# Seven quarter products for five of the 22 pairs of an MLP's first product

## The chip, the cores and the metric

One Trainium2 chip, one of its cores. The metric is device microseconds of one execution, from the kernel's first instruction to its last output. Engines are called by these names: TensorE (PE in the profile, with PEld for its weight loads), VectorE (DVE), ScalarE (ACT), GpSimd (POOL), SyncE (SP, which issues DMAs).

## The reference, cut to what matters

One layer of an encoder over 512 tokens of 1024 channels: four token mixers, a cross-attention, then a gated MLP. The change is in the MLP:

```python
hf = _rms_norm(x, norm_ffn_pre)                       # (512, 1024)
u = _dwconv_causal(hf @ w_up, ffn_dw) + ffn_dw_b      # w_up (1024, 5632), width-3 taps over tokens
u_g, u_v = jnp.split(u, 2, axis=-1)                   # 2816 gate, 2816 value channels
yff = (jax.nn.silu(u_g) * u_v) @ w_down               # w_down (2816, 1024)
x = x + _rms_norm(yff, norm_ffn_post)
```

All is float32, and the products keep more than one pass of TensorE would: each operand x is split into a rounded high part and a low part x - high, and a product is the sum of three (high·high, high·low, low·high).

## The kernel before, in words

The kernel writes out its work as a list of jobs (`all_jobs`), which `run_blocks` takes in order: a job loads a block of weights (`load_raw`, on SP's queue, two buffers `wr`), splits it (`split_weights`: ScalarE casts the high part `wh`, L190; VectorE subtracts for the low part `wl`, L191; four buffers each) and runs a body of matmuls. Three jobs are fetched ahead of the body that runs. The program's own scheduler then sets each engine's order, so an engine's rows are not in the order of the code.

**The first MLP product** (`up_jobs`). The 2816 gate and 2816 value channels are 22 pairs of blocks of 128 channels; block n is pair j = n // 2, gate or value i = n % 2. A block is 8 steps k of 128 input channels by 3 passes = 24 matmuls of 128x128 weights against 128x512 tokens (`channel_major`, `mm3`; every matmul is recorded at L232), summed in one PSUM bank. Then `done`: ScalarE starts the width-3 convolution out of PSUM (L1557), VectorE adds the other two taps (L594, `taps`), and after the value block ScalarE takes a tanh (L1561) and VectorE makes silu(gate)·value out of it in two instructions (L1562, L1564). The first four blocks run on 256 tokens at a time, since the second half of the tokens is normalized last (`norm_task`, which turns each 128 tokens to channels on TensorE, L236, and splits them into `hth` and `htl`, L155 and L156).

**The second MLP product** (`down_jobs`) already takes seven products of quarters for eight, in two phases over 11 double pairs q. For it GpSimd sums quarters of the activations (`activation_sums`, L566 to L569, four instructions for each q, as soon as pair 2q + 1 is done), and VectorE sums quarters of the weights during the first product (class `Sums`, L542 to L545, four instructions for each q), loading from and storing to DRAM on ScalarE's DMA queue (L538, L549).

The banks of PSUM: two each of `mm`, `av`, `sc`, `tr`. The first product uses `mm` and `av` in turn, and `sc` for two of the first four blocks; `tr` and `sc` are otherwise free while it runs.

Of the kernel before, what the change touches and what calls it, by code (L numbers as in the profile page):

```python
# [17 lines left out]
F32 = mybir.dt.float32  # L18
# [20 lines left out]
HALF_SHIFT = 16  # L39
BIG = -float(2.0 ** 100)  # L40
# [43 lines left out]
def hybrid_layer(ctx: ExitStack, tc: tile.TileContext, a: dict, out: bass.AP):  # L84
# [146 lines left out]
    def matmul(ps, lhs, rhs, start, stop):  # L231
        PE.matmul(ps, lhs, rhs, start=start, stop=stop)  # L232
        bg.clock += max(int(math.prod(rhs.shape[1:])), 256) * 0.00042
# [52 lines left out]
    def to_channels(y_t, act, t):  # L286

        sl = slice(t * P, (t + 1) * P)
        for half in range(2):
# [4 lines left out]
            split(ps.rearrange("p (k c) -> p k c", k=4), act[0][:, ks, sl], act[1][:, ks, sl])  # L294

# [994 lines left out]
    def norm_task(t, ms, scaled, src, gain, act):  # L1290
# [5 lines left out]
        if act is ns.hx:  # L1296
            load_x(t + 2)
        y_t = normed(ns.work, ns.out[t], [gain], ns.work.tile([P, D], F32, tag="nt", name="nt", bufs=2), ns.normed)
        yield 2.5, 7.0
        to_channels(y_t, act, t)  # L1300
# [7 lines left out]
    def open_mix_out():  # L1308
        close(m2)
        ns.res_, resp = new_pool("res", False)  # L1310
        ns.xr, ns.normed = None, []
        ns.out = [resp.tile([P, D], F32, name=f"res{t}") for t in range(NT)]
# [113 lines left out]
    def open_cross():  # L1426
        close(ns.mix_)
        ns.xp_, ns.xp = new_pool("xp", True)
        ns.xq = (ns.xp.tile([P, 4, S], F32R, name="xqh"), ns.xp.tile([P, 4, S], F32R, name="xql"))
        ns.pt = {}  # L1430
        ns.xp_gap = True
# [72 lines left out]
    def open_cross_out():  # L1504
# [5 lines left out]
        ns.hf = new_ht()  # L1510

# [26 lines left out]
    def open_ffn():  # L1538
        bg.drain("n1")
        close(ns.work_)  # L1540
# [4 lines left out]
        ns.quart = [(ns.fp.tile([P, 4, S // 2], F32, tag=f"qa{q}", name="qa"),  # L1545
                     ns.fp.tile([P, 3, S // 2], F32, tag=f"qb{q}", name="qb")) for q in range(NF // 2)]
        ns.post = ns.fp.tile([P, D], F32, name="g_ffn")
        G.dma_start(ns.post, a["norm_ffn_post"][0].partition_broadcast(P))

    def up_jobs():  # L1550
        st, held = {}, []

        def done(j, i, ps):
            if i == 0:
                st[j] = ns.fp.tile([P, 2, S], F32, tag="c", name="c", bufs=2)
            c, ch = st[j], i * NF + j
            st["first"] = A.activation(c[:, i], ps, AF.Identity, bias=pc("fb", ch), scale=pc("fdw2", ch)).ins  # L1557
            st["taps"] = taps(c[:, i], ps, lambda k: pc("fdw01", k * 44 + ch), 3).ins
            if i == 1:
                th = ns.fp.tile([P, S], F32, tag="th", name="th")  # L1560
                A.activation(th, c[:, 0], AF.Tanh, scale=0.5)  # L1561
                V.scalar_tensor_tensor(th, th, 1.0, c[:, 0], ALU.add, ALU.mult)  # L1562
                x = ns.quart[j // 2]
                V.scalar_tensor_tensor(x[j % 2][:, 0:2].rearrange("p a b -> p (a b)"), th, 0.5, c[:, 1],  # L1564
                                       ALU.mult, ALU.mult)
                if j % 2:
                    activation_sums(*x, G)


        for n in range(2 * NF):  # L1570
            def body(hi, lo, n=n):
                j, i = divmod(n, 2)
                if n > 3:
                    ps = bank()
                    channel_major(ps, (hi, lo), ns.hf)
                    done(j, i, ps)

                    q = n // 3 - 2
                    if 0 <= q < NF // 2:
                        with tc.issue_after(st["taps" if n % 3 == 0 else "first"]):  # L1580
                            (ns.sums.add, ns.sums.store, ns.sums.load)[n % 3](q + 2 * (n % 3 == 2))
                    return
                if n == 0:
                    bg.drain("n0")
                ps = bank(("mm", "sc")[n % 2])
                (channel_major if n else by_pass)(ps, (hi, lo), ns.hf, slice(0, S // 2))
# [233 lines left out]
```

## Time and profile before

| | |
|---|---|
| median of 3 runs | 1055.36 us (1055.04 to 1056.72) |
| the profiled execution, its own time | 1055.79 us |
| span of its profile | 1054.0 us |
| mean granted clock of TensorE | 0.997 |
| first MLP product, by TensorE | 695.8 to about 946 us |
| second MLP product and the end | about 946 to 1054 us |
| DMA during the first product (750 to 900 us) | 225 GB/s, 69% of the DMA engines' time |

A row of an engine's timeline has the start in us, the length in us, engine, line, operation, what is written and read, the shape, and in brackets how long the engine was idle before and what ended that. Instructions of one engine overlap a little: the next starts before the one ahead of it has ended. In the chain of waits a row is a start, a length and what ran; x24 stands for 24 matmuls in a row. Times in the text are from the span's start.

### The profile page before, as it was taken

The numbers are of one execution on the slowest core, as the hardware profiler recorded it, in microseconds if no ns is written. First come the engines' busy times: TensorE is split into PE (matmuls) and PEld (weight loads), VectorE is DVE, ScalarE is ACT, GpSimd is POOL, SyncE is SP. The second block draws the span as 40 slices with busy tenths as digits, with TensorE's granted clock in tenths as the row PEclk, the third lists the DMA queues.
The fourth block names the chain that finished last, engine by engine and source line by source line (L and its number), as shares of the span: only waits on it lengthen the run. The fifth ranks groups of instructions, "written<-read, shape, count | busy, mean of one in ns | idle before, by whom it ended". The sixth has DMA issues, their size and how long they took to land.

```text
span 1054.0 us, 14559 instructions
## 1 busy us (share of the span) xinstructions
PE 1041.7 (99%) x5295; PEld 886.8 (84%) x5295; DVE 807.1 (77%) x1280; ACT 501.9 (48%) x823; POOL 184.3 (17%) x309
## 2 busy tenths in 40 slices
PE   9999999999999999999999999999999999999996
PEld 8888888888888988888888899998888888888885
DVE  6899997668667467867487798777878777777795
ACT  5322222277465365655444566554333333355661
POOL 4000000300231233433011031121112111111001
PEclk9999999999999999999999999999999999999998
DMA  8854434742342353232359644135576676626662
GB/s 276 282 168 102 103 100 142 193 109 81 116 140 82 100 161 101 80 100 85 96 172 284 207 132 126 60 111 190 186 243 229 214 233 215 196 81 211 210 188 80
DMA packets 165373, 163.08 MB, mean 155 GB/s; under 512 B 6527, under 2 KB 136172, under 8 KB 165045
## 3 DMA queue, kind: packets, MB, share of 16 engines
q1 hardware_dynamic: 152995, 119.91, 38.0%
q0 software_dynamic: 5824, 19.03, 6.2%
q10 hardware_dynamic: 6482, 23.21, 5.7%
q8 instruction: 42, 0.69, 0.3%
q14 instruction: 30, 0.25, 0.1%
HBM read 139.03 MB, written 23.09 MB: 154 GB/s over the span
## 4 chain that ended last, share of the span: by engine, by line
PE 99%; DVE 0%; ACT 0%; issue 0%; POOL 0%; POOLq 0%; DVEq 0%; ACTq 0%
PE ps_mm L232 51%; PE ps_av L232 31%; PE ps_sc L232 8%; PE ps_tr L232 4%; PE ps_tr L236 2%; PE ps_mm L442 1%; PE ps_av L442 1%; PE ps_mm L384 0%; PE ps_sc L389 0%; DVE o L1710 0%; PE ps_tr L426 0%; POOL st_m L270 0%; POOLq L1816 0%; ACT hth L155 0%; ACT hth L432 0%
## 5 line engine op out<-in xcount | busy, mean ns | idle before, releaser
L190 ACT CAST wh<-wr 128x1024 fp32r<-128x1024 f32 (+1 forms) x142 | 148.8, 1049 | 273.3 <-PE ps_mm L232 175.0
L191 DVE TENSOR_TENSOR wl<-wr,wh 128x1024 fp32r<-128x1024 f32 (+1 forms) x142 | 178.5, 1258 | 79.0 <-ACT wh L190 78.8
L232 PE MATMUL ps_mm<-hth,wh 128*128 128x512 f32 (+1 forms) x592 | 221.1, 380 | 0.2 <-ACT hth L155 0.2
L232 PE MATMUL ps_mm<-htl,wh 128*128 128x512 f32 (+1 forms) x592 | 220.7, 379 | 0.0
L232 PE MATMUL ps_mm<-hth,wl 128*128 128x512 f32 (+1 forms) x592 | 220.6, 379 | 0.0
L232 PE MATMUL ps_av<-htl,wh 128*128 128x512 f32 (+1 forms) x352 | 131.8, 374 | 0.0
L232 PE MATMUL ps_av<-hth,wh 128*128 128x512 f32 (+1 forms) x352 | 131.8, 374 | 0.0
L232 PE MATMUL ps_av<-hth,wl 128*128 128x512 f32 (+1 forms) x352 | 131.6, 374 | 0.0
L232 PEld LDWEIGHTS ps_mm<-hth,wh 128*128 128x128 f32 x592 | 109.6, 188 | 20.4 <-ACT hth L155 0.8
L232 PEld LDWEIGHTS ps_mm<-hth,wl 128*128 128x128 f32 x592 | 109.5, 188 | 20.1
L232 PEld LDWEIGHTS ps_mm<-htl,wh 128*128 128x128 f32 x592 | 109.6, 188 | 19.7
L665 DVE SCALAR_TENSOR_TENSOR y<-y,par,y 128x482 f32<-128x482 f32 (+29 forms) x120 | 83.3, 735 | 0.1
L232 PEld LDWEIGHTS ps_av<-hth,wl 128*128 128x128 f32 x352 | 66.1, 188 | 11.9
L232 PEld LDWEIGHTS ps_av<-hth,wh 128*128 128x128 f32 x352 | 66.2, 188 | 11.8
L232 PEld LDWEIGHTS ps_av<-htl,wh 128*128 128x128 f32 x352 | 66.0, 188 | 11.7
L1613 DVE TENSOR_TENSOR wl<-dw,wh 128x1024 fp32r<-128x1024 f32 x32 | 40.2, 1262 | 13.3 <-ACT wh L1612 13.1
L1612 ACT CAST wh<-dw 128x1024 fp32r<-128x1024 f32 x32 | 33.4, 1051 | 23.4 <-PE ps_tr L232 7.9
L1058 POOL TENSOR_SCALAR fbias<-ck,cq 128x128 f32<-128x128 f32 (+3 forms) x32 | 28.2, 888 | 63.0 <-DVE st L1065 59.7
L1561 ACT ACTIVATE th<-c 128x512 f32<-128x512 f32 x22 | 13.9, 632 | 48.0 <-DVE c L594 48.0
L155 ACT CAST pth<-ps_tr 128x512 fp32r<-128x512 f32 (+3 forms) x56 | 23.5, 448 | 24.7 <-PE ps_tr L236 24.6
L594 DVE SCALAR_TENSOR_TENSOR c<-ps_mm,par,c 128x510 f32<-128x510 f32 (+1 forms) x44 | 32.8, 744 | 0.7
L156 DVE TENSOR_TENSOR ptl<-ps_tr,pth 128x512 fp32r<-128x512 f32 (+3 forms) x56 | 27.5, 512 | 5.9 <-ACT pth L155 5.4
(493 smaller groups left out, 2132.5 us busy)
## 6 DMA issues: line engine op xcount, KB each, us to landing
wr<-in_w_up SPq DMA_DIRECT2D x44, 512.0 KB
wr<-in_w_in SPq DMA_DIRECT2D x38, 512.0 KB
wr<-in_w_gate SPq DMA_DIRECT2D x32, 512.0 KB
wp<-in_w_down ACTq DMA_DIRECT2D x22, 512.0 KB
sums<-wp ACTq DMA_DIRECT2D x22, 512.0 KB
dw<-sums SPq DMA_DIRECT2D x44, 256.0 KB
wr<-in_w_branch SPq DMA_DIRECT2D x16, 512.0 KB
wide<-in_w_out SPq DMA_DIRECT2D x12, 512.0 KB
```

What stands on the lines that cost most here:

```text
L155: A.copy(hi, ps)
L156: V.tensor_tensor(lo, ps, hi.bitcast(F32), ALU.subtract)
L190: order(A.copy(hi, raw[:, :n]))
L191: low.tensor_tensor(lo, raw[:, :n], hi.bitcast(F32), ALU.subtract)
L232: PE.matmul(ps, lhs, rhs, start=start, stop=stop)
L236: PE.transpose(ps, x, ident[:n, :n])
L442: keep(PE.matmul(banks[c][:, :S // 2], w[p == 1][:, k, c * P:(c + 1) * P], ht[p == 2][:, i * 4 + k, :S // 2], start=(i, p, k) == (0, 0, 0) ...
L594: ins = V.scalar_tensor_tensor(dst[:, s:], src[:, :S - s], w(k), dst[:, s:], ALU.mult, ALU.add)
L665: ins = V.scalar_tensor_tensor(dst[:, s:], src[:, :S - s], pc("conv_dw", k * 4 + j), dst[:, s:], ALU.mult, ALU.add)
L1058: G.tensor_scalar(bias[:, :w], ck[j][:, :w], -1.0, cq[:, qt, head:head + 1], ALU.mult, ALU.add)
L1612: A.copy(hi, x)
L1613: V.tensor_tensor(lo, x, hi.bitcast(F32), ALU.subtract)
```

## The change

**Pairs 5, 8, 11, 14 and 17** (`SEVEN_AT`) are computed in another way (`seven_jobs`). The pair's weights are seen as two rows, gate (A11, A12) and value (A21, A22), each cut into halves of 4 steps k; the tokens as four quarters B, cut by channel halves and token halves. Seven products of a weights' quarter with a tokens' quarter give the pair, with sums S1 to S4 of the weights and T1 to T4 of the tokens. A product is 4 steps by 3 passes = 12 matmuls against 256 tokens, into `sc` and `tr`; four of the seven go on adding into the same bank after ScalarE copied out the sum so far. The pair after (6, 9, 12, 15, 18) is done in the old way, its matmuls woven between the seven products, and pairs 7, 10, 13 and 16 stand between.

For it are added, for each of the five pairs: VectorE sums S1 to S4 (4 instructions of 128x512), one more split of 128x1024 (S1, S2) and one of 128x512 (S4), three additions out of PSUM of 128x256, and four copies out of PSUM of 128x256 on ScalarE. The splits of the pair's own two blocks stay, of (A11, A12) and of (S3, A22). Its raw weights come into a ring of 7 buffers (`dw`) that the sums of `w_down` use too; before, those had 4.

**The tokens' terms.** `norm_task` now also copies the turned tokens out of PSUM (`plain`, ScalarE, two copies of 128x512 for each of the four token tiles), and VectorE makes T1 to T4 from them (`token_terms`, 4 instructions of 128x1024) and splits them (`split_terms`, four more and four casts). T1 to T4 stand where the residual stood, so each of its four tiles goes to DRAM on SP's queue (`kept`, 512 KB each) and comes back during the second product (`reload`).

**Smaller edits.** For every pair, silu on ScalarE and one multiplication on VectorE take the place of tanh and two; ScalarE loads another function table once for it. The sums of `w_down` go through GpSimd's DMA queue in place of ScalarE's. GpSimd's sums of activations all come after pair 18 (`quart_sums`). The splits of the activations in the second product are two instructions of half the size in place of one.

```diff
+SEVEN_AT = (5, 8, 11, 14, 17)
...
     split(ps.rearrange("p (k c) -> p k c", k=4), act[0][:, ks, sl], act[1][:, ks, sl])
+    if plain is not None:
+        A.copy(plain[half][:, :, sl], ps.rearrange("p (k c) -> p k c", k=4))
...
+    def token_terms():
+        b11, b12, b21, b22 = (ns.plain[k][:, :, i * S // 2:(i + 1) * S // 2] for k in range(2) for i in range(2))
+        ns.terms = t1, t2, t3, t4 = [term_tile(i) for i in range(4)]
+        V.tensor_tensor(t1, b12, b11, ALU.subtract)
+        V.tensor_tensor(t2, b22, t1, ALU.subtract)
+        V.tensor_tensor(t3, b22, b12, ALU.subtract)
+        V.tensor_tensor(t4, b21, t2, ALU.subtract)
...
-                th = ns.fp.tile([P, S], F32, tag="th", name="th")
-                A.activation(th, c[:, 0], AF.Tanh, scale=0.5)
-                V.scalar_tensor_tensor(th, th, 1.0, c[:, 0], ALU.add, ALU.mult)
...
-                V.scalar_tensor_tensor(x[j % 2][:, 0:2].rearrange("p a b -> p (a b)"), th, 0.5, c[:, 1],
-                                       ALU.mult, ALU.mult)
+            A.activation(c[:, 0], c[:, 0], AF.Silu)
+            V.tensor_tensor(ns.quart[j // 2][:, j % 2 * 2:j % 2 * 2 + 2].rearrange("p a b -> p (a b)"), c[:, 0],
+                            c[:, 1], ALU.mult)
...
+            ns.sums = Sums(w_down, NF // 2, lambda: ring(name="wp"), G, "sums")
...
+            def first_weights():
+                weights(("A11", "A12"), g)
+                with tc.issue_after(st["taps"]):
+                    V.tensor_tensor(su[:, :S], v[:, :S], v[:, S:], ALU.add)
+                V.tensor_tensor(su[:, S:], su[:, :S], g[:, :S], ALU.subtract)
+                V.tensor_tensor(v[:, :S], g[:, :S], v[:, :S], ALU.subtract)
+                V.tensor_tensor(s4, g[:, S:], su[:, S:], ALU.subtract)
...
+            def first(_):
+                product(x["x"], "A11", old(0, 0))
+                A.copy(u[:, 0, 0], x["x"][:, :S // 2])
+                product(x["w"], "A12", old(1, 0))
+                add(u[:, 0, 0], x["w"])
+            def gate_first(hi, lo):
+                x["n"] = bank(), (hi, lo)
+                half_sums(*x["n"], range(4))
+            def second(_):
+                product(x["x"], "S2", ns.terms[1], False)
+                A.copy(kept["u"][:, 1, 0], x["x"][:, :S // 2])
+            def third(_):
+                product(x["v"], "S3", ns.terms[2])
+                half_sums(*x["n"], range(4, NK))
+                done(n, 0, x["n"][0])
+                product(x["x"], "S1", ns.terms[0], False)
+                A.copy(u[:, 1, 1], x["x"][:, :S // 2])
+                add(u[:, 1, 1], x["v"])
+            def value(hi, lo):
+                half_sums(ps, (hi, lo), range(4))
+                product(x["x"], "S4", old(1, 1), False)
+                A.copy(u[:, 0, 1], x["x"][:, :S // 2])
+                half_sums(ps, (hi, lo), range(4, NK))
+                done(n, 1, ps)
+                product(x["v"], "A22", ns.terms[3], False)
+                add(u[:, 1, 0], x["v"])
+                for i in range(2):
+                    first_and_taps(c, j, i, u[:, i].rearrange("p a b -> p (a b)"))
+                gated(c, j)
...
+            split_to(hi[:, :S], lo[:, :S], flat(ns.quart[q][:, 2 * phase:2 * phase + 2]))
+            split_to(hi[:, S:], lo[:, S:], new)
...
+            if (phase, q, job) == (1, 2, 0):
+                reload()
```

How instructions stand on VectorE in the middle of the first product, before (`wl<-wr` is the low part of a block's weights, `c` the convolution, `th` and `qb` the gate, `wp` the sums of `w_down`):

```order
L1562 SCALAR_TENSOR_TENSOR th<-th,c 128x512
L191 TENSOR_TENSOR wl<-wr,wh 128x1024
L594 SCALAR_TENSOR_TENSOR c<-ps_av,par_403,c 128x510
L594 SCALAR_TENSOR_TENSOR c<-ps_av,par_403,c 128x511
L542 TENSOR_TENSOR wp<-wp 128x512
L1564 SCALAR_TENSOR_TENSOR qb<-th,c 128x512
L543 TENSOR_TENSOR wp<-wp 128x512
L544 TENSOR_TENSOR wp<-wp 128x512
```

And at such a place now (`su`, `wv`, `s_8109` are the sums S1 to S4, `u` the additions out of PSUM):

```order
L1693 TENSOR_TENSOR su<-wv 128x512
L192 TENSOR_TENSOR wl<-wr,wh 128x1024
L1686 TENSOR_TENSOR u<-u,ps_sc 128x256
L546 TENSOR_TENSOR wp<-wp 128x512
L1694 TENSOR_TENSOR su<-su,wg 128x512
L1695 TENSOR_TENSOR wv<-wg,wv 128x512
L547 TENSOR_TENSOR wp<-wp 128x512
L192 TENSOR_TENSOR wl<-wr,wh 128x1024
L1696 TENSOR_TENSOR s_8109<-wg,su 128x512
L597 SCALAR_TENSOR_TENSOR c<-ps_av,par_403,c 128x510
L548 TENSOR_TENSOR wp<-wp 128x512
L597 SCALAR_TENSOR_TENSOR c<-u,par_403,c 128x510
```

Sums S1 to S4 and additions have come between the splits and the taps; a stretch of three pairs, which is one of the five and the two behind it, is 38 instructions on VectorE.

On VectorE at the start of the MLP, behind the last token tile's split, stand now the terms T1 to T4 (`t_7000` and on) ahead of the next blocks' low parts, and their splits (`t_7139`) between the first taps:

```order
L1575 TENSOR_TENSOR t_7002<-plain 128x1024
L1574 TENSOR_TENSOR t_7001<-plain,t_7000 128x1024
L1576 TENSOR_TENSOR t_7003<-plain,t_7001 128x1024
L192 TENSOR_TENSOR wl<-wr,wh 128x1024 x2
L597 SCALAR_TENSOR_TENSOR c<-ps_mm,par_403,c 128x510
L597 SCALAR_TENSOR_TENSOR c<-ps_sc,par_403,c 128x510
L157 TENSOR_TENSOR t_7139<-t_7000,t_7138 128x1024
```

Before, the two `wl` came straight behind the last token tile's split.

On TensorE, in a stretch of seven products (`t_7146` is T3, `t_7142` is T2; the rows of 128x512 into `ps_mm` are the neighbour pair's gate block):

```order
L233 MATMUL ps_mm<-hth,wl 128x512
L233 MATMUL ps_sc<-t_7146,wh 128x256
L233 MATMUL ps_sc<-t_7147,wh 128x256
L233 MATMUL ps_mm<-hth,wh 128x512
L233 MATMUL ps_mm<-htl,wh 128x512
L233 MATMUL ps_mm<-hth,wl 128x512
L233 MATMUL ps_sc<-t_7142,wh 128x256
```

Where there were 24 matmuls of 512 columns of one block after the other, runs of 256 columns now alternate with runs of 512: one such stretch turns from 256 columns to 512 six times.

More of the change, by code (lines that the diff above doesn't have):

```diff
@@ L1599, in down_jobs @@
+        j = 0
+        while j < NF:
+            yield from (seven_jobs if j in seven else plain_jobs)(j)
+            j += 2 if j in seven else 1
+        for f, q in steps:
+            yield then(lambda f=f, q=q: f(q))
     def down_jobs():
@@ L1644, in weights @@
             if (phase, q) == (1, pairs - 1):
-                hi, lo = (ns.fp.tile([P, D], F32R, tag="dw", name="dwr", bufs=4) for _ in range(2))
+                hi, lo = (ring(F32R, "dwr") for _ in range(2))
             else:
```

217 lines of the change are left out of this document (170 added, 47 removed).

## The prediction

> **What bounds the kernel now.** I read the page first: who is busy, and what the chain that ended last consists of. Then TensorE's waits, the chain in order of time, and last the stretch that the change touches, by engine.
>
> ```profile
> span 1054.0 us, 14559 instructions
> PE 1041.7 (99%) x5295; PEld 886.8 (84%) x5295; DVE 807.1 (77%) x1280; ACT 501.9 (48%) x823; POOL 184.3 (17%) x309
> PE 99%; DVE 0%; ACT 0%; issue 0%; POOL 0%; POOLq 0%; DVEq 0%; ACTq 0%
> ```
>
> ```profile
> PE ps_mm L232 <- ACT hth L155: 0.2, 1, 0.2
> ```
>
> The second fence is the whole answer on who TensorE waited for from 700 us to the end: once, 0.2 us. In the MLP the time is that of the matmuls, so an edit gains only what it takes from TensorE, and costs only where it makes TensorE wait. What a matmul costs is read from the chain, where a run's length is counted from its start to the next run's start:
>
> ```profile
> 698.59 1.25 PE ps_sc L232 x11
> ...
> 702.55 2.83 PE ps_mm L232 x24
> 705.38 2.83 PE ps_sc L232 x24
> 708.21 0.45 PE ps_tr L236 x4
> 708.66 0.02 issue
> 708.68 0.59 ACT hth L155
> 709.27 0.04 issue
> ...
> 753.56 5.44 PE ps_mm L232 x24
> ```
>
> At 753 us a block of 24 matmuls of 512 columns takes 5.44 us, 0.2267 us each. The first blocks run on 256 columns: 24 in 2.83 us, 0.118 each, a little more than half (0.1133). Only short runs are at half: 11 in 1.25 us, 0.114.
>
> ```profile
> 750.00:900.00 150.00, 150.00 (x663) 124.23 (x662) 118.68 (x148) 55.18 (x68) 25.94 (x27) 1.00 0.69 225
> ```
>
> In the middle of the first product TensorE is busy all of the 150 us at a granted clock of 1.00, VectorE 118.7 us or 79%, ScalarE 37%, GpSimd 17%. VectorE is the only other engine that is near anything.
>
> **The change part by part.** *Matmuls.* A pair is 2 blocks by 24 matmuls = 48 x 0.2267 = 10.88 us. Seven products by 12 = 84 matmuls of 256 columns are 84 x 0.118 = 9.91 us, or 84 x 0.114 = 9.58 by the short run. I take 0.118, as the two longest runs have it: 0.97 us less for a pair, **4.9 us for five**; 6.5 us at the other end. [...]
>
> *Turns between the widths.* The seven products alternate with 512-column runs, six turns to 512 in each of five stretches. The nearest rows are at 667 us, where such a turn happens without transposes:
>
> ```profile
> 668.08 0.28 PE L232 MATMUL ps_av<-pth,vxl 128*128 128x256 f32 x1
> 668.20 0.40 PE L232 MATMUL ps_mm<-wh,oxl 128*128 128x512 f32 x1
> 668.44 0.40 PE L232 MATMUL ps_mm<-wh,oxh 128*128 128x512 f32 x1
> 668.67 0.39 PE L232 MATMUL ps_mm<-wl,oxh 128*128 128x512 f32 x1
> 668.90 0.39 PE L232 MATMUL ps_mm<-wh,oxl 128*128 128x512 f32 x1
> ```
>
> The three starts behind the turn are 0.24, 0.23 and 0.23 apart, together 0.70 where 3 x 0.2267 = 0.68: 0.02 us for a turn, 30 turns 0.6 us. Bounds are 0 and, were all 96 wide matmuls of a stretch at 0.23, 5 x 96 x 0.0033 = 1.6 us.
>
> *VectorE in a stretch of three pairs* (one by seven products, two plain). TensorE needs 2 x 10.88 + 9.91 = 31.7 us for it. VectorE's durations are these groups, from 760 to 900 us:
>
> ```profile
> L191 DVE TENSOR_TENSOR wl<-wr,wh 128x1024 fp32r<-128x1024 f32 x26 | 33.8, 1301 | 20.1 <-ACT wh L190 20.1
> L594 DVE SCALAR_TENSOR_TENSOR c<-ps_av,par,c 128x510 f32<-128x510 f32 x13 | 9.7, 743 | 0.0
> L1562 DVE SCALAR_TENSOR_TENSOR th<-th,c 128x512 f32<-128x512 f32 x13 | 9.0, 690 | 6.8 <-ACT th L1561 6.8
> L544 DVE TENSOR_TENSOR wp<-wp 128x512 f32<-128x512 f32 x9 | 8.3, 923 | 0.2
> L542 DVE TENSOR_TENSOR wp<-wp 128x512 f32<-128x512 f32 x8 | 5.5, 682 | 0.0
> ```
>
> and, for an addition of 128x256 out of PSUM, the one near the end:
>
> ```profile
> 1043.62 0.42 DVE L1731 TENSOR_TENSOR o<-o,ps_av 128x256 f32<-128x256 f32 x1
> ```
>
> Now 7 low parts of 128x1024 (9.1 us), one of 128x512 (0.69), four sums S (2.76), three additions (1.26), 12 taps (8.9), 3 gates (2.07, one instruction in place of two, which saves 0.69 a pair) and two of the sums of `w_down`, 8 instructions (5.5 to 7.4): **30.2 to 32.2 us** by durations. The lengths overlap, though:
>
> ```profile
> 776.21 1.23 DVE L191 TENSOR_TENSOR wl<-wr,wh 128x1024 fp32r<-128x1024 f32 x1
> 777.36 0.69 DVE L545 TENSOR_TENSOR wp<-wp 128x512 f32<-128x512 f32 x1
> 777.96 1.53 DVE L594 SCALAR_TENSOR_TENSOR c<-ps_av,par,c 128x510 f32<-128x510 f32 x2
> 779.52 0.69 DVE L1564 SCALAR_TENSOR_TENSOR qa<-th,c 128x512 f32<-128x512 f32 x1
> ```
>
> From start to start a low part takes 1.15 us and an instruction of 512 columns 0.60, two taps at most 1.56. By starts, with 0.35 for an addition: 8.05 + 0.6 + 2.4 + 1.05 + 6 x 1.56 + 1.8 + 4.8 = **28.1 us, 89% of 31.7**. I take the starts, because GpSimd's additions are gone from these stretches (they all come after pair 18), and VectorE's long rows (1301 against 1225 to 1230, 923 against 682) are the ones beside GpSimd's. Cover for what VectorE does late: weights are split three blocks ahead, some 16 us, and a bank of PSUM is wanted again four blocks on. I went through one stretch with these starts and TensorE's order: each low part is ready 5 to 12 us before its matmuls, and the one close wait of the new kind, the last product on the addition that empties its bank, has 7.2 us between the product that it needs and itself. I price it at **0**, up to 2 us a stretch if that cover is thinner.
>
> ScalarE gets four copies, a cast of 512 columns and one of 1024 in such a stretch: at 0.58 for 512 columns out of PSUM (the cast below) at most 4.1 us in 31.7, beside its 37%. Its function table is loaded once, where it has idle time. Price 0.
>
> *The start of the MLP.* VectorE gets T1 to T4 and their splits, eight instructions of 128x1024, 8 x 1.15 = 9.2 us; ScalarE eight copies of 0.58 and four casts of 1024 columns.
>
> ```profile
> 708.68 0.58 ACT L155 CAST hth<-ps_tr 128x512 fp32r<-128x512 f32 x1 [4.30 <-PE ps_tr L236]
> ```
>
> ```profile
> 709.30 1.29 DVE L156 TENSOR_TENSOR htl<-ps_tr,hth 128x512 fp32r<-128x512 f32 x2 [2.71 <-ACT hth L155]
> 714.71 1.23 DVE L191 TENSOR_TENSOR wl<-wr,wh 128x1024 fp32r<-128x1024 f32 x1 [4.12 <-ACT wh L190]
> 715.85 0.74 DVE L594 SCALAR_TENSOR_TENSOR c<-ps_mm,par,c 128x510 f32<-128x510 f32 x1
> ```
>
> ScalarE was idle 4.3 us ahead of the cast that TensorE waits for at 709.27, so the third tile's two copies (1.2 us) lie there; the last tile's come behind the cast. VectorE was idle 4.1 us from 710.6 to 714.7: the four T (4.6 us), which can begin when the last copy ends at about 711, fill that, and the fifth block's low part moves from 714.7 to about 715.6, needed at 720.6 (709.3 and 96 matmuls by 0.118). The split T's then push the seventh block's low part to about 727, and the eighth's to 729.5; TensorE comes to them at 731.5 and 732. Price **0**, with a margin of some 3 us; without it up to 4 us once. SP's queue has the residual's stores (512 KB each) and the first raw pair ahead of the seventh block's load: 1 MB at 225 GB/s is 4.7 us, which eats the same margin.
>
> *GpSimd's queue.* The sums' loads wait there behind their stores. The nearest rows are its own loads of 512 KB:
>
> ```profile
> xin<-in_x POOLq DMA_DIRECT2D x4, 512.0 KB, 6.0
> g_ffn<-in_norm_ffn_post POOLq DMA_DIRECT2D x1, 512.0 KB, 4.2
> ```
>
> A sum is loaded four steps, about 21 us, ahead of its addition; store and load landed one behind the other are 12 us. Price 0. *GpSimd's additions* all come after pair 18:
>
> ```profile
> L566 POOL TENSOR_TENSOR qa<-qa,qb 128x256 f32<-128x256 f32 x7 | 5.9, 844 | 68.2 <-DVE qb L1564 68.2
> L569 POOL TENSOR_TENSOR qb<-qb,qa 128x256 f32<-128x256 f32 x6 | 7.9, 1315 | 0.5
> ```
>
> 44 of them are 37 to 58 us, from some 33 us (three pairs) ahead of the second product; its double pairs are wanted 5.44 us apart from there on, so the last is due 87 us after the first could begin. Price 0. *The second product* gets four loads of 512 KB more on SP's queue, and halved splits cost VectorE 0.05 us each: both under TensorE, which has no wait there. Price 0.
>
> **The sum**, against the profiled execution's own 1055.8 us (its span of 1054.0 and 1.8 around it): -4.9 + 0.6 = -4.3, so 1051.5. The median of the runs is 1055.4, 0.4 less than the profiled one; so I say **1051.1 us**, 0.4% faster.
>
> **The rivals.** *Half-width matmuls at half price* (0.114, no turns): -6.5, so 1048.9. For it speak the run at 698.6, against it the two longer ones. *The gain is eaten at the start*: the seventh and eighth blocks' weights come 3 us late, behind T1 to T4 and the raw pair on SP's queue: 1054.1; it decides where the low part of the seventh block comes later than 731.5. *VectorE becomes the bound in the five stretches*, which ends slower: its 38 instructions at the durations beside GpSimd, 32.2 us, and 3 us in which its queue stands at a low part whose buffer TensorE still reads (the block before ends at 11 us of the stretch) make 35.2 us against TensorE's 31.7. That is 3.5 x 5 = 17.5 us, so 1068.6; it decides from the point where VectorE's work and those waits exceed 31.7 us. For it speaks the 30.2 to 32.2 us by durations; against it the overlap, and that weights are three blocks ahead. [...]
>
> **How the numbers follow.** My forecast has 0.60, half price 0.14, eaten at the start 0.12, VectorE bound 0.10, late sums 0.04. Faster by over 0.2% (2.1 us, about what a measurement of this kernel can tell from no change) is 0.74; of the third case most lies within 0.2%, so same 0.12; slower 0.14. The range reaches from 1048.6 (half price) to 1055.6 (the start and 1 us a stretch lost), and leaves out what is slower.
>
> **What would show it.** In the changed profile: 84 matmuls at 0.118 between the wide ones; TensorE's waits still under 1 us from 700 us on; VectorE at 85 to 90% from 760 to 900 us with idle time in front of low parts; TensorE's last block of the first product some 4 us earlier. Waits of TensorE for `wl` or `u` in the stretches would prove the cover wrong, a wait near 731 us the start, and an addition `wp` behind a DMA the queue.

## The result, and the profile after

The changed kernel takes 1054.37 us (median of 20 runs, 1052.70 to 1055.88), the kernel before 1055.70 us beside it (20 runs, 1054.88 to 1057.19): a ratio of 0.9984, 95% interval 0.9977 to 0.9991. That is 1.3 us less, where 4.3 were forecast. The profiled run took 1053.96 us.

The page of the changed kernel, its span, the engines' busy time and the engines' shares of the chain:

```profile
span 1052.2 us, 15086 instructions
PE 1037.9 (99%) x5475; PEld 889.7 (85%) x5475; DVE 833.5 (79%) x1333; ACT 526.6 (50%) x888; POOL 216.2 (21%) x353
PE 91%; DVE 5%; issue 1%; ACT 1%; DMA 1%; POOL 0%; POOLq 0%; DVEq 0%; SPq 0%; ACTq 0%
```

TensorE's share of the chain fell from 99 to 91%: followed back, it now leaves TensorE and runs for a stretch through VectorE. Where, TensorE's waits from 700 us to the end say (engine, tile, line, who ended the wait; total, times, longest):

```profile
PE ps_sc L233 <- ACT hth L1808: 2.0, 1, 2.0
PE ps_mm L233 <- DVE c L597: 1.8, 1, 1.8
PE ps_av L233 <- DVE c L597: 1.1, 1, 1.1
PE ps_mm L233 <- ACT hth L156: 0.2, 1, 0.2
```

Before, only the last row was there (as L155). The three new ones stand at 929.8, 940.8 and 944.5 us, around the start of the second product at 935.4: 4.9 us in all. In the five stretches there is none, as the chain shows. In it 785.80, 817.43 and 849.06 are the starts of three stretches' first products; the rows of the first stretch are its 84 matmuls of 256 columns:

```profile
785.80 1.42 PE ps_sc L233 x12
787.21 1.41 PE ps_tr L233 x12
...
791.37 0.24 PE ps_sc L233 x2
...
792.30 2.50 PE ps_sc L233 x22
...
798.00 1.42 PE ps_sc L233 x12
...
805.10 1.41 PE ps_sc L233 x12
...
806.75 1.37 PE ps_sc L233 x12
...
817.43 1.42 PE ps_sc L233 x12
...
849.06 1.42 PE ps_sc L233 x12
```

and the middle of the first product by engine (busy us of PE, PEld, DVE, ACT, POOL):

```profile
750.00:900.00 150.00, 150.00 (x854) 131.75 (x853) 126.23 (x172) 68.98 (x97) 35.58 (x53) 1.00 0.68 221
```

Three pairs, one of them by seven products, take 31.63 us against 6 x 5.44 = 32.64. Most runs of 12 matmuls of 256 columns take 1.41 or 1.42 us, 0.118 each; 22 in a row take 2.50, 0.114 each. The 84 together take 9.77 us. VectorE is busy 84% of 750 to 900 us. The sums' transfers have changed queues, q10 being ScalarE's and q0 GpSimd's (packets, MB, share of the DMA engines' time); first before, then after:

```profile
q0 software_dynamic: 5824, 19.03, 6.2%
q10 hardware_dynamic: 6482, 23.21, 5.7%
```

```profile
q0 software_dynamic: 12160, 42.10, 12.1%
q10 hardware_dynamic: 146, 0.14, 0.0%
```

**Where the time went.** Each trace has three marks: the start of TensorE's last seven matmuls ahead of the MLP's own (694.38 us before, 695.27 after; the MLP's first follows 1.45 us later in both), the start of the second product (938.36 before, not about 946 as the table of the profile before has it; 935.41 after), and the end of the last VectorE instruction (1047.68 and 1049.06). Between them lie, in us:

| trace | first product | second product | from the last VectorE instruction to the end of the span |
|---|---|---|---|
| before | 243.98 | 109.32 | 6.3 |
| after | 240.14 | 113.65 | 3.1 |
| after, less before | -3.8 | +4.3 | -3.2 |

So the first product gained 3.8 us, the second lost 4.3, and the end of the program, which is no part of the MLP, gave 3.2. The first mark itself lies 0.9 us later in this trace of the changed kernel, but at 694.14 in its second trace; in the 16 traces it lies anywhere from 694.14 to 696.21. The measured gain is the end of the program; what the seven products gave was lost again, and the MLP alone takes 0.5 us more than before in this trace.

What is lost is seen where VectorE (DVE) and GpSimd (POOL) run beside each other, in the timeline of the changed kernel. L192 is a low part of weights, L1647 to L1650 are GpSimd's additions, L597 a tap:

```profile
914.95 1.18 POOL L1648 TENSOR_TENSOR t<-qa 128x256 f32<-128x256 f32 x1
915.47 5.93 DVE L192 TENSOR_TENSOR wl<-wr,wh 128x1024 fp32r<-128x1024 f32 x1
916.11 0.73 POOL L1647 TENSOR_TENSOR t<-qa 128x256 f32<-128x256 f32 x1
916.80 2.12 POOL L1649 TENSOR_TENSOR qa<-t,qa 128x256 f32<-128x256 f32 x3
918.89 1.43 POOL L1650 TENSOR_TENSOR t<-qa 128x256 f32<-128x256 f32 x2
921.32 1.52 DVE L597 SCALAR_TENSOR_TENSOR c<-ps_mm,par,c 128x510 f32<-128x510 f32 x2
```

A low part takes 1.22 us; this one 5.93. While it stands, GpSimd does six additions without a gap, each 0.7 us, and the low part ends 1.1 us after the last of them. The taps behind it start at 921.3, and VectorE stays late: 19 us on, a silu of ScalarE still waits for taps. ScalarE's timeline, with the idle time in brackets:

```profile
940.77 0.63 ACT L1600 ACTIVATE c<-c 128x512 f32<-128x512 f32 x1 [3.82 <-DVE c L597]
...
943.81 0.61 ACT L1808 CAST hth<-qa 128x512 fp32r<-128x512 f32 x1
```

The cast at 943.81 is the one that TensorE waits for at 944.5. It reads quarters that VectorE and GpSimd had written by 919 us; it stood behind the silu in ScalarE's order.

### The profile page after: what moved, and what is told of

Its sections match the earlier page's. It is cut to its first block, busy times and chain, and to the rows that moved or that the text cites. A ratio compares the mean times of both kernels' runs of the same rounds, so it can differ in the third digit from the quotient of the medians.

```text
span 1052.2 us, 15086 instructions
## 1 busy us (share of the span) xinstructions
PE 1037.9 (99%) x5475; PEld 889.7 (85%) x5475; DVE 833.5 (79%) x1333; ACT 526.6 (50%) x888; POOL 216.2 (21%) x353
## 3 DMA queue, kind: packets, MB, share of 16 engines
q0 software_dynamic: 12160, 42.10, 12.1%
## 4 chain that ended last, share of the span: by engine, by line
PE 91%; DVE 5%; issue 1%; ACT 1%; DMA 1%; POOL 0%; POOLq 0%; DVEq 0%; SPq 0%; ACTq 0%
PE ps_mm L233 46%; PE ps_av L233 26%; PE ps_sc L233 12%; PE ps_tr L233 5%; PE ps_tr L237 2%; DVE wl L192 1%; DVE c L597 1%; DMA wide<-in_w_out 1%; DMA xs<-in_x 0%; DVE wl L1809 0%; ACT wh L191 0%; DVE wp L548 0%; DVE nt L282 0%; DVE wp L545 0%; POOL st_r L272 0%
## 5 line engine op out<-in xcount | busy, mean ns | idle before, releaser
L191 ACT CAST wh<-wr 128x1024 fp32r<-128x1024 f32 (+1 forms) x132 | 138.2, 1049 | 236.8 <-PE ps_mm L233 130.0
L192 DVE TENSOR_TENSOR wl<-wr,wh 128x1024 fp32r<-128x1024 f32 (+1 forms) x132 | 170.7, 1295 | 62.4 <-ACT wh L191 62.2
L233 PE MATMUL ps_mm<-hth,wh 128*128 128x512 f32 (+1 forms) x552 | 205.7, 380 | 0.2 <-ACT hth L156 0.2
L233 PE MATMUL ps_mm<-htl,wh 128*128 128x512 f32 (+1 forms) x552 | 205.3, 379 | 0.0
L233 PE MATMUL ps_mm<-hth,wl 128*128 128x512 f32 (+1 forms) x552 | 205.0, 379 | 0.0
L233 PE MATMUL ps_av<-hth,wh 128*128 128x512 f32 (+1 forms) x312 | 116.4, 373 | 1.1 <-DVE c L597 1.1
L233 PE MATMUL ps_av<-htl,wh 128*128 128x512 f32 (+1 forms) x312 | 116.3, 373 | 0.0
L233 PE MATMUL ps_av<-hth,wl 128*128 128x512 f32 (+1 forms) x312 | 116.2, 372 | 0.0
L233 PE MATMUL ps_mm<-y8b,wh 128*128 128x512 f32 x96 | 30.3, 393 | 0.0
L233 PE MATMUL ps_mm<-y,wh 128*128 128x512 f32 x96 | 30.2, 393 | 0.0
```

The costliest lines, as they stand in the source:

```text
L191: order(A.copy(hi, raw[:, :n]))
L192: low.tensor_tensor(lo, raw[:, :n], hi.bitcast(F32), ALU.subtract)
L233: PE.matmul(ps, lhs, rhs, start=start, stop=stop, skip_group_check=more)
```

## The experiments

All ratios are to the kernel before, run beside each; the kernel before itself once more gave 1056.57 us against 1056.27, ratio 0.9999 (0.9990 to 1.0008), and its trace again 6.3 us at the end.

> The kernel before once more, for a second look at its end: in its first profile the span ended 6.3 us after the last vector instruction, in that of the change 3.1 us after. If the landing of the last outputs differs from run to run, this profile shows another distance; if the change shortens it, again about 6 us. The ratio of times should be 1.000 either way.

**The additions left out**, in `quart_sums`:

```diff
-                G.tensor_tensor(two[:, 0], x[:, 1], x[:, 3], ALU.add)
-                G.tensor_tensor(two[:, 1], x[:, 0], x[:, 1], ALU.subtract)
-                G.tensor_tensor(x[:, 1], two[:, 0], x[:, 0], ALU.subtract)
-                G.tensor_tensor(one, x[:, 2], x[:, 1], ALU.subtract)
-                ns.quart_sums[q] = two, one
+                ns.quart_sums[q] = x[:, 2:4], x[:, 3]
```

> Leaves out GpSimd's 44 additions of activations (the second product then reads quarters in place of their sums). Theory A, the additions hold up VectorE after pair 18 and TensorE waits for VectorE 4.9 us: the three waits go and the time is about 1049.5 us, 0.994 of before. Rival B, VectorE has too much to do there by itself: the waits stay, about 1054.4 us, 0.999 of before. VectorE's low parts between 890 and 925 us would be 1.2 us each under A and stretched still under B.

Measured 1047.93 us, ratio 0.9921 (0.9908 to 0.9933). The three waits are gone, the low parts of weights (L192) between 890 and 925 us take 1.21 to 1.23 us each, and the second product is back at 109.32 us. So the additions cost all of the lost 4.3 us and more; VectorE without them has room. How late they make it is told by its last row on pair 19, the gate's product: counted from the first mark it starts at 224.7 us here, and at 234.5 in the changed kernel.

**The additions paced**: each group waits for a ScalarE instruction that follows a block of TensorE, so that six groups stand beside pairs 19 to 21 and five in the second product.

```diff
-                            quart_sums(min(2 * (2 * (j - seven[-1] - 2) + i) + 2, (j + i) // 2))
+                            quart_sums(2 * (j - seven[-1] - 2) + i + 1, st["first"])
+            if phase == 0 and q:
+                ns.more_sums(min(q + 6, pairs), parts["cast"])
```

> The same additions, but each double pair's four wait for a cast of ScalarE that follows a block of TensorE, so that one double pair is summed per block of pairs 19 to 21 and the rest in the second product. Theory A: VectorE is held up by at most 4 additions per 5.4 us, within its room, and the time is 1049.5 to 1051 us, 0.994 to 0.996 of before. Rival B: no change from the changed kernel, about 1054.4 us. If the pace is too slow, TensorE waits in the first phase of the second product for sums, which no theory here claims.

Measured 1052.90 us, ratio 0.9967 (0.9954 to 0.9980): a part comes back, less than theory A's 1049.5 to 1051. The waits for taps are gone, but a cast in ScalarE's order now waits 3.5 us for a late sum, and TensorE behind it:

```profile
PE ps_sc L233 <- ACT hth L1811: 2.3, 1, 2.3
```

**The sums on ScalarE's queue again** (`lambda: ring(name="wp"), G` becomes `A`):

> The sums of the last weights through ScalarE's DMA queue, as before the change; all else as changed. Theory A: the additions still come in one batch, 1054 us within 1 us, 0.998 to 0.999 of before. Rival Q, GpSimd's queue is at fault, since its DMAs and additions stand in one line and a late store delays them: the waits go, about 1050 us, 0.995 of before.

Measured 1055.97 us, ratio 0.9995 (0.9986 to 1.0004), and 6.3 us at the end of its trace: without GpSimd's queue no gain is left that can be told from none. Rival Q's 1050 fell, but theory A's 1054 is missed too, and the two parts must be told apart. The end is 3.2 us longer than the changed kernel's; the MLP, from the first mark to the last VectorE instruction, takes 351.71 us, 2.1 less than in the changed kernel (353.79) and 1.6 less than before (353.30). TensorE's new waits are 2.0 and 1.1 us, and between 912 and 946 us GpSimd is busy 17.60 us, 15.06 in the changed kernel. So with the same additions on GpSimd the loss is smaller here; whether GpSimd's DMA instructions among its additions (0.57 or 0.58 us each there) do it, or only the way in which the rows then meet, isn't shown.

**The queue alone**: the kernel before with one word changed.

```diff
-    ns.sums = Sums(w_down, NF // 2, lambda: ns.fp.tile([P, D], F32, tag="dw", name="wp", bufs=4), A,
+    ns.sums = Sums(w_down, NF // 2, lambda: ns.fp.tile([P, D], F32, tag="dw", name="wp", bufs=4), G,
```

> The kernel before, with one part of the change alone: the 22 loads and 22 stores of the last weights' sums are issued on GpSimd's queue in place of ScalarE's. Nothing else differs. Theory A (the end of the program after the last VectorE instruction is shorter when ScalarE's queue carries little: it was 6.3 us in the kernel before and in the changed kernel with its sums on ScalarE's queue, and 3.1 to 3.3 us in the three kernels with the sums on GpSimd's queue): the end is 3.1 to 3.3 us, everything up to the last VectorE instruction stays, and the time falls by about 3.2 us, to 1052.5, ratio 0.997. Rival (the shorter end belongs to something else in the changed kernel, such as the reload of the kept rows): the end stays 6.3 us and the ratio is 1.000. Second rival (the transfers wait on GpSimd's queue and come late): TensorE gets new waits in the second product and the ratio is above 1.000 whatever the end does.

Measured 1053.54 us, ratio 0.9976 (0.9967 to 0.9985), no new wait in the MLP, end 3.2 us. This one word gives as much as the whole change. That it is ScalarE's light load, as theory A had it, is a separate claim; with SyncE's queue (`A` becomes `SP`) ScalarE's carries as little:

> The kernel before with the last weights' sums issued on SyncE's queue in place of ScalarE's. ScalarE's queue then carries as little as in the changed kernel (0.14 MB), and GpSimd's as little as in the kernel before (19.03 MB). Theory A (the end of the program is short when ScalarE's queue carries little): the end after the last VectorE instruction is 3.1 to 3.3 us, as with GpSimd's queue. Rival (it is short when GpSimd's queue carries much): it stays 6.3 us. The time itself may go either way, since 22 stores now stand in SyncE's order ahead of the loads of the first product's weights and wait there for VectorE: 1052.5 if that costs nothing.

Measured 1055.69 us, ratio 0.9997 (0.9988 to 1.0006), end 6.3 us with q10 at 0.14 MB: theory A fell. What shortens the end is GpSimd's queue. Its amount or its late use? `Sums` takes the queue by the pair of rows:

```diff
+        def on(self, q):
+            return self.queue if self.queue is SP else G if q >= self.pairs - 3 else A
```

and `q < self.pairs - 3` in the other run.

> The kernel before with the sums of the last three of the 11 pairs of rows on GpSimd's queue (12 of the 44 transfers, the latest in time); the other eight stay on ScalarE's. Theory R (the end of the program is short when GpSimd's queue was last used late): the end after the last VectorE instruction is 3.1 to 3.3 us, as in the run with all 44 there, and the time 1052.5 to 1053.5. Theory V (it is short when GpSimd's queue has carried much, 42 MB in place of 19): it stays 6.3 us and the time stays 1056.

> The kernel before with the sums of the first eight of the 11 pairs of rows on GpSimd's queue (32 of the 44 transfers, the earliest), and the last three on ScalarE's. Theory R (the late use of GpSimd's queue shortens the end): 6.3 us, 1056. Theory V (the amount on that queue shortens it): 3.1 to 3.3 us, 1052.5 to 1053.5, or something between if it goes by degrees.

The last three on GpSimd: 1057.05 us, ratio 1.0010 (1.0001 to 1.0019), 25.32 MB on q0, end 7.3 us. The first eight: 1052.52 us, ratio 0.9964 (0.9951 to 0.9977), 35.81 MB, end 2.9 us. Late use is refuted. The end goes with the amount, but not by degrees: 19.03 MB go with 6.3, 25.32 with 7.3, 35.81 with 2.9, 42.10 with 3.1 to 3.3. The run with the larger amount also had the earlier transfers; no run tells these two apart.

**Four pairs in place of five** (`SEVEN_AT = (5, 8, 11, 14)`), which moves the additions three pairs forward:

> The changed kernel with four pairs by seven quarter products in place of five (pair 17 is computed plainly); GpSimd's 44 additions then begin after pair 15 instead of after pair 18. Theory A1 (each pair by seven products gives 1.0 us, and GpSimd's additions cost their 4.9 us of TensorE waits only because VectorE, held up by them, has no time left to catch up before the second product): the additions end some 30 us earlier, the three waits of 1.1, 1.8 and 2.0 us shrink to under 2 us in all, and the time is 1050.5 to 1053. Rival A2 (the loss is the same wherever the additions stand): the waits stay near 4.9 us at an earlier place or the same, and the time is 1.0 us above the changed kernel's, 1055.4. Rival C (each pair by seven products costs rather than gives): the time falls by a part of the sums' 1 us and no wait changes.

Measured 1049.59 us, ratio 0.9941 (0.9929 to 0.9954): 4.8 us faster than with five, and no wait of TensorE but the old 0.2 us. The additions are as many, and they stretch VectorE's rows here too (the last of the four sums `wp` takes 0.84 us in the mean, 0.69 without additions). But GpSimd is busy with them some 30 us earlier (24.49 us of 849 to 880), VectorE has that time to catch up, and the gate product of pair 19 starts at 225.1 us. Rival A2 fell, and the time is even below theory A1's 1050.5 to 1053. Rival C fell with the next run: there five pairs take 1.0 us less from the first mark to the last VectorE instruction than these four (348.65 against 349.64).

**The additions on VectorE itself** (the four lines with `V` for `G`):

> The changed kernel with the 44 additions of the activations' quarters on VectorE in place of GpSimd. One of them should take some 0.35 to 0.42 us there (half of the 0.69 us that a 128x512 row with two inputs in SBUF takes without GpSimd beside it), 15 to 18 us in all. Theory A (it is the holding up of VectorE's own rows beside GpSimd's that costs): the rows of the weights' split go back from up to 5.93 us to 1.22, but 15 to 18 us of work are added; in the run without the additions VectorE was idle for 7.7 us of 880 to 912 and 2.6 us of 912 to 929, so that the additions just don't fit ahead of the second product: TensorE waits of 2 to 6 us, time 1051 to 1055. Rival (only the amount of VectorE's work counts, and the additions beside it cost it less than their own 15 to 18 us): waits of 8 us and more, time 1057 or above. Third outcome (they fit, since half of them are needed only later): waits under 1 us, time 1049.

Measured **1048.08 us, ratio 0.9927 (0.9913 to 0.9940)**, no wait but the 0.2: the third outcome. The second product takes 109.37 us, though the silu, the halved splits, the reloads and the queue are all as changed, so none of these is behind the lost 4.3 us. The same two stretches ahead of the second product by engine (busy us of PE, PEld, DVE, ACT, POOL), in the changed kernel, then without the additions, then with them on VectorE:

```profile
880.00:912.00 32.00, 32.00 (x184) 28.07 (x183) 28.43 (x31) 12.24 (x17) 26.69 (x30) 1.00 0.74 243
912.00:929.00 17.00, 16.70 (x74) 13.46 (x72) 16.75 (x16) 7.37 (x10) 10.30 (x13) 1.00 0.39 134
```

```profile
880.00:912.00 32.00, 32.00 (x183) 28.08 (x182) 24.30 (x35) 13.48 (x19) 2.68 (x5) 1.00 0.90 304
912.00:929.00 17.00, 17.00 (x77) 14.08 (x76) 14.39 (x20) 8.40 (x12) 1.07 (x2) 1.00 0.71 236
```

```profile
880.00:912.00 32.00, 32.00 (x183) 28.05 (x183) 28.62 (x55) 13.26 (x19) 2.67 (x5) 1.00 0.67 212
912.00:929.00 17.00, 17.00 (x77) 14.08 (x76) 17.00 (x28) 8.49 (x11) 1.06 (x2) 1.00 0.53 155
```

In the 49 us VectorE did 55 rows without the additions, 47 beside GpSimd's, though it was busy 6.5 us longer, and 83 with the additions among its own. The gate product of pair 19 starts at 229.2 us, 4.4 later than without the additions, and that costs nothing yet. The low parts of weights between 890 and 925 us are back at 1.22 or 1.23 us. On VectorE an addition takes 0.42 us:

```profile
926.21 0.42 DVE L1649 TENSOR_TENSOR qa<-t,qa 128x256 f32<-128x256 f32 x1
```

**The additions spread on GpSimd**: two groups in the stretches (the free buffer of T4), five beside pairs 19 to 21, four in the second product's first phase, the last addition of each group later still.

```diff
+                if j in seven[-2:]:
+                    quart_sums(1 + (j == seven[-1]), st["first"])
+            if phase == 0 and q:
+                ns.more_sums(min(q + 7, pairs), parts["cast"])
+                ns.late_sums(min(max(2 * (q - 4), 0), pairs), parts["cast"])
```

> The changed kernel with the same 44 additions on GpSimd, spread out: two of the 11 groups stand beside the seventh products of pairs 14 and 17, in the buffer of a term that is free by then; five stand beside pairs 19 to 21, one to each block of TensorE; four in the first phase of the second product; and the last addition of each group, which only the second phase needs, comes in the first phase's second half. Each group waits for a ScalarE instruction that follows a block of TensorE, so that it cannot run early. Theory A (the burst of additions holds up VectorE just ahead of the second product, where it has no time to catch up): with at most 15 additions in the 32 us ahead of the second product in place of 44, the three waits of 4.9 us shrink to under 1.5 us in all, and the time is 1049 to 1051.5, ratio 0.994 to 0.996. Rival (each addition costs VectorE what it costs, wherever it stands, and VectorE has no slack): the waits keep their 4 to 5 us at other places, time 1053 to 1055.

Measured 1053.06 us, ratio 0.9974 (0.9965 to 0.9982). Theory A's size missed; the rival's time is met, though its reason is not (VectorE had slack, as the runs with four pairs and with the additions on VectorE show). The burst only moved. From 938.9 us eight low parts of activations stand beside ten additions, and the two engines take turns:

```profile
938.90 1.23 DVE L1829 TENSOR_TENSOR htl<-qa,htl 128x512 fp32r<-128x512 f32 x1
940.05 1.23 DVE L1829 TENSOR_TENSOR htl<-t,htl 128x512 fp32r<-128x512 f32 x1
941.20 1.23 DVE L1829 TENSOR_TENSOR htl<-qa,htl 128x512 fp32r<-128x512 f32 x1
```

1.15 us from start to start in place of 0.60. The last taps come late by it, and TensorE waits 2.9 us for them:

```profile
PE ps_av L233 <- DVE c L597: 2.9, 1, 2.9
```

**The additions kept, but unread:**

```diff
-                G.tensor_tensor(x[:, 1], two[:, 0], x[:, 0], ALU.subtract)
+                G.tensor_tensor(two[:, 0], two[:, 1], x[:, 0], ALU.subtract)
-                ns.quart_sums[q] = two, one
+                ns.quart_sums[q] = x[:, 2:4], x[:, 1]
```

> The changed kernel with GpSimd's 44 additions kept in their place and number, but with results that nothing reads: the second product reads quarters of the activations in place of the sums (this leaves the sums out of the output), and the third addition of each group writes its own buffer. So nothing can wait for a late sum, and all that the additions can do is to stand beside VectorE's rows. Theory A (they hold up VectorE's rows that read two operands in SBUF, and the taps and splits behind those come late): VectorE's gate products between 906 and 950 us are 4 to 10 us later than in the run without the additions, TensorE still waits 2 to 5 us for taps and casts, and the time is 1050 to 1054. Rival B (the second product waits for the sums themselves, which GpSimd ends late): no wait above 0.6 us, and the time is that without the additions, 1048.

Measured 1049.84 us, ratio 0.9943 (0.9930 to 0.9956). One wait is left, 1.6 us for a cast behind a silu behind taps, and the gate product of pair 19 starts at 229.4 us. Rival B fell: standing beside VectorE is enough to make it 4.7 us late and to bring a wait, with nothing that reads a sum. The changed kernel's own trace agrees: from 880 to 1000 us neither TensorE nor VectorE nor ScalarE waits there for a GpSimd instruction. But theory A's size is missed: the wait and the time lie just under its bounds, 1.9 us above the run without additions, where the changed kernel is 6.4 above it. The additions don't stand quite in their place either. The fourth of each group needn't wait for the third, and GpSimd is further on (31.11 us busy in 880 to 912, against 26.69), and the rows meet in another order; the longest row of VectorE is one of 3.33 us.

**The additions on VectorE and spread**, as in the spread run but with `V` in place of `G` and no pacing:

> The changed kernel with the 44 additions on VectorE, two of the 11 groups ahead of the stretches in the buffer of a term that is free by then, and the last addition of each group free to come in the second product's first phase. With all 44 on VectorE after pair 18 TensorE had no wait left and the time was 1048.1 us, though VectorE was busy all of 912 to 946. Theory A (TensorE bounds this part as soon as GpSimd's additions are gone, and VectorE's work has room there): nothing more is to be had, 1047.5 to 1048.8. Rival (VectorE's full 34 us still cost something that the waits don't show): 1046 to 1047.

Measured 1047.82 us, ratio 0.9920 (0.9906 to 0.9934): no more than with the additions after pair 18. TensorE bounds this part again, with no wait but the 0.2 us.

**The changed kernel once more:**

> The changed kernel itself, once more. If the waits of TensorE ahead of the second product come from how GpSimd's and VectorE's rows happen to fall beside each other, then the sum of the three waits (4.9 us in the first trace) and the long row of VectorE (5.93 us at 915) will be of another size in this trace, with the same rows named, and the times spread over about 3 us as before. If they come from the order of the program alone, they come back within 0.3 us. Time 1053 to 1055.5 either way.

Measured 1053.79 us, ratio 0.9977 (0.9968 to 0.9987). The waits are 2.0, 1.8 and 0.9 us, and the long row comes again, 5.93 us at 914.13. So these rows belong to the order of the program; the trace shows a loss of clock besides, told below.

## Why the prediction was off

The mechanism of the gain was right, the sum of the prices not. That the time still lies inside the stated range is luck: it was brought there by the end of the program, which no step had foreseen. With the end as it was before, the changed kernel would be at some 1057.6 us (an estimate, 1054.4 + 3.2).

*Five pairs, -4.9 us, and turns, +0.6.* Right, and the gain a little under-priced. With the additions on VectorE the MLP from the first mark to the last VectorE instruction takes 348.65 us (before 353.30): 4.65 less, against 4.3. In a stretch the 84 matmuls of 256 columns take 9.77 us in place of the 9.91 that was taken, since not every run of them is at 0.118. The 96 wide ones take the other 21.86, 0.10 more than 96 x 0.2267; six turns at 0.02 were to cost 0.12.

*VectorE in the stretches, 0; the start of the MLP, 0; the sums' transfers on GpSimd's queue, 0.* Right in so far as TensorE waits in none of these places. The rivals for them, "eaten at the start", "VectorE the bound in the five stretches" and "late sums" (of `w_down`, on GpSimd's queue), did not come, nor did half price. No run shows the late transfers that the 0.04 of "late sums" stands for: in the changed kernel the load of a sum landed 5.1 us after its issue (median), and from 700 us on no addition into `wp` on VectorE waited for one. But the queue wasn't without effect: with ScalarE's queue in its place the MLP was 2.1 us shorter and the end 3.2 longer.

*GpSimd's additions, "Price 0".* **This is the step that failed.** It asked only whether the sums arrive in time. What they do to VectorE beside them was named earlier, under VectorE in a stretch, where VectorE's long rows were put down to GpSimd and the additions were said to be gone from the stretches because "they all come after pair 18". They had moved to the 49 us just ahead of the second product, and there they were not priced. The rows quoted for the prediction were a warning: 1301 against 1225 ns, 923 against 682, with GpSimd at 17%. With GpSimd at 26.69 of 32 us the cost is 5.1 us: from the first mark to the last VectorE instruction the changed kernel takes 353.79 us, with the same additions on VectorE 348.65. In the changed kernel's trace, between 890 and 922 us, four of the five low parts (up to 5.93 us in place of 1.22) and the four sums (up to 2.63 in place of 0.69) are stretched, and so are the four taps that read `u` (0.90 to 1.22 in place of 0.74), with GpSimd's additions beside them; the taps there that read PSUM keep their 0.74 or 0.75.

*The second product, "under TensorE, which has no wait there. Price 0".* It fell with that step. No wait before the change meant no wait while VectorE was on time.

*The end of the program.* It stood in no step, being the same in the forecast as before; it gave 3.2 us. The sum of what was found is -4.65 (gain, by the run with the additions on VectorE) + 5.1 (the additions on GpSimd) + 0.9 (the first mark) - 3.2 = -1.8, the difference of the two spans; the medians differ by 1.3.

Open: why the end depends on what GpSimd's queue has carried, with a jump between 25 and 36 MB; and what sets the size of the 5.1 us, since the kernel with unread additions and the one with ScalarE's queue have the additions in another order and lose less.

## What to carry to other kernels

When work is put on an idle engine, price what it does to the engine beside it, at the place where it will stand, and not only whether its results are in time; a busy engine with 10 us to spare did the same additions for less (0.42 us each among VectorE's own rows) than an idle one beside which a low part took 5.93 us in place of 1.22. Here the same additions cost nothing that could be seen where the held engine had some 30 us more to catch up (the run with four pairs), and 5.1 us just ahead of the second product. And compare the end of the program, behind the last instruction, as a term of its own: here it hid that the MLP had become no faster.

## What the runs showed of the hardware

*A row stood as long as six of the other engine's rows.* In the spread run the two engines took turns (1.15 us from start to start). In the changed kernel a row of VectorE stands through six additions (5.93 us in place of 1.22, in both traces). It happens the other way round, too: a GpSimd addition stands 6.86 us in place of 0.73 beside VectorE's low parts (between 1.8 and 2.8 us in the second trace, by its windows of 1 us). What decides between turns and a long wait isn't shown. By its end at 958.41, less 0.73, the addition got through at about 957.7, where one low part ends and the next begins (an estimate from these rows):

```profile
951.55 6.86 POOL L1647 TENSOR_TENSOR two<-qa 128x256 f32<-128x256 f32 x1 [11.73 <-DVE qa L1601]
```

```profile
956.59 1.22 DVE L1809 TENSOR_TENSOR wl<-dw,wh 128x1024 fp32r<-128x1024 f32 x1
957.78 1.18 DVE L1809 TENSOR_TENSOR htl<-qa,htl 128x512 fp32r<-128x512 f32 x1
```

*Behind a wait of 2.0 us TensorE's clock stood at 0.50 for some 3.4 us, in one of two traces.* In the second trace of the changed kernel the matmuls behind the wait of 2.0 us take 0.43 us each in place of 0.227. Its chain, four matmuls to a row, and windows of 1 us (third number from the end: granted clock):

```profile
943.14 1.29 PE ps_sc L233 x4
944.42 1.71 PE ps_tr L233 x4
946.13 1.61 PE ps_mm L233 x4
```

```profile
944.00:945.00 1.00, 1.00 (x4) 0.79 (x3) 1.00 (x3) 1.00 (x3) 0.00 (x0) 0.55 0.77 279
945.00:946.00 1.00, 1.00 (x4) 0.72 (x3) 1.00 (x3) 1.00 (x3) 0.00 (x0) 0.50 0.24 84
946.00:947.00 1.00, 1.00 (x4) 0.81 (x3) 1.00 (x2) 1.00 (x2) 0.00 (x0) 0.50 0.51 111
947.00:948.00 1.00, 1.00 (x4) 0.81 (x4) 1.00 (x3) 0.30 (x1) 0.00 (x0) 0.75 1.00 401
```

The four windows hold 3.4 us at a clock of 0.50 and the rest at 1.00, if those are the only two values. Behind the waits of 2.3 us (paced) and 2.9 us (spread) it is as long, with such windows at 0.87, three times 0.50 and 0.92, and at 0.88, three times 0.50 and 0.91; behind the same 2.0 us in the first trace and in the run with ScalarE's queue, and 1.6 with unread additions, it stays at 1.00. That is some 1.7 us (half of 3.4) which come or don't. The lists of runs point the same way: of the changed kernel's 20 runs, the 11 with a mean clock of 0.995 to 0.997 have spans of 1052.5 to 1054.1 us, the 9 with 0.998 or 0.999 have 1050.9 to 1052.2, but for one of 1053.4. Not all spread is that, though: the kernel before, with no such wait, spreads over 2.3 us. Why the same wait of 2.0 us is followed by the lower clock in one trace and not in two others isn't shown.

*The end of the program* took 6.3 us behind the last VectorE instruction in four traces, 7.3 in one and 2.9 to 3.3 in the other eleven. It isn't the last store: in windows of 1 us (last two columns: share of the DMA engines, GB/s) the transfers end within about 2 us of that instruction in the kernel before and in the changed one, but before there are 4 us more without any transfer, after little over 1:

```profile
1049.00:1050.00 1.00, 0.00 (x0) 0.00 (x0) 0.00 (x0) 0.00 (x0) 0.00 (x0) 0.50 0.14 46
1050.00:1051.00 1.00, 0.00 (x0) 0.00 (x0) 0.00 (x0) 0.00 (x0) 0.00 (x0) 0.50 0.00 0
...
1053.00:1054.00 1.00, 0.00 (x0) 0.00 (x0) 0.00 (x0) 0.00 (x0) 0.00 (x0) 0.50 0.00 0
```

```profile
1050.00:1051.00 1.00, 0.00 (x0) 0.00 (x0) 0.00 (x0) 0.00 (x0) 0.00 (x0) 0.50 0.56 193
1051.00:1052.00 1.00, 0.00 (x0) 0.00 (x0) 0.00 (x0) 0.00 (x0) 0.00 (x0) 0.50 0.00 0
```
